# Three pads that move the operands of the MLP products in SBUF

## The chip, the cores and the metric

The kernel runs on one core of a Trainium2 chip. The metric is the device time of one execution in microseconds; three runs of the kernel before took 2766.51, 2768.69 and 2768.96 us, so the median is 2768.69 us. All times below come from these runs and from one profiled execution.

## The reference

Two transformer blocks follow each other on one sequence of 1024 tokens with 1024 channels, in float32. The first block adds to x the sum of three gated attention branches (sliding window, sparse with an exact top 256, and cross-attention to a memory of 256 tokens), then an MLP, and a norm. The second block is modulated by a conditioning vector; its mixer is a two-way mLSTM with four heads beside a multi-scale pooling, and it too ends in an MLP. The two MLPs are the part that the pads are named after:

```python
h = rmsnorm(x, g_mlp[l])
hid = jnp.square(jax.nn.relu(jnp.einsum("bsd,df->bsf", h, w_mlp_in[l])))
x = x + jnp.einsum("bsf,fd->bsd", hid, w_mlp_out[l])
...
h = _modulate(_rmsnorm(x, g_ffn[l]), sh2, sc2)
a = jnp.square(jax.nn.relu(jnp.einsum('bsd,df->bsf', h, w_ff1[l])))
x = x + gt2[:, None, :] * jnp.einsum('bsf,fd->bsd', a, w_ff2[l])
```

d is 1024 and f is 4096.

## The kernel before

Every large product is done in three: an operand is split into a high part (float32r) and the rest, and the kernel adds hi x hi, hi x lo and lo x hi in one PSUM bank. In `gemm_T` these are the lines L418, L419 and L420. A weight unit (128 contraction rows, 128 output channels, tiles wh and wl) is the stationary operand; the activations, transposed so that tokens lie along the free dimension, are the moving one, 512 tokens at a time. A moving operand is thus 128 partitions by 512 values of 4 bytes, 2048 bytes of each partition. The second mixer issues the same three products at L1301 to L1303 (`gemm2`), and the gates that are computed in advance, between the attention's steps, at L268 to L270.

The activations stand in these tiles: h_hi and h_lo, the normed input of a block or of an MLP, 8 channel blocks of 512 tokens, one pair for each half of the tokens (the first half in pool hA, the second in hB, or in hBp while hB holds the residual); hid_hi and hid_lo, the hidden layer of an MLP, rings of four tiles each in pool hidp; and for smaller products o_s, om and od (the outputs of the three attention branches), m (the merged branches) and y (the second mixer's output).

An MLP (`mlp`) goes in eight chunks of 512 hidden channels. In a chunk, four weight units give four hid tiles of both halves (8 channel blocks x 2 halves x 3 products each), and eight output blocks then take 4 x 2 x 3 products each from them. ScalarE takes the relu out of PSUM, VectorE squares it, and both split it; VectorE adds each output block into the residual stream x. Weights arrive by SP's DMA queue in tile wr and are split by ScalarE (L131) and VectorE or GpSimd (L132) into rings of three wh and wl tiles.

Pools are stacks: pools on the left side of SBUF grow upward from the constants (cst), hA and hB directly above; pools on the right (the weights' wp above all) grow downward. A pool that is opened takes the next free address, so whatever lies below a tile sets its address. Instructions are written out in a fixed order, and the tile framework puts the waits in by the tiles' addresses.

Of the kernel before, what the change touches and what calls it, by code (L numbers as in the profile page):

```python
# [19 lines left out]
P = 128  # L20
# [40 lines left out]
def block_kernel(ctx, tc, x, mem, positions, g_mix, w_in, b_gate, sinks, g_mem, w_mem_kv, w_proj_swa, w_proj_dsa,  # L61
# [65 lines left out]
    # ------------------------------------------------------------------ weights  # L127
# [12 lines left out]
    # ------------------------------------------------------------------ inputs needed first  # L140
# [6 lines left out]
    # ------------------------------------------------------------------ natural rmsnorm + transposes  # L147
# [32 lines left out]
    # ------------------------------------------------------------------ rope tables  # L180
# [52 lines left out]
    # ------------------------------------------------------------------ gates in advance, between the attention's steps  # L233
# [10 lines left out]
    def gates_ahead(todo):  # L244
        """tanh of half the gates' logits, into DRAM; a piece of three products at a time"""
# [55 lines left out]
    # ------------------------------------------------------------------ natural GEMM pieces  # L301
# [17 lines left out]
    def rope_nat(pool, acc, t, nh, dst=None):  # L319
        """acc: PSUM [P, nh*64] -> rotated [P, nh, 64] in SBUF"""  # L320
        av = acc.rearrange("p (h two j) -> p h two j", h=nh, two=2)
        a = pool([P, nh, 2, 32], tag="rp_a", bufs=2)
        V.tensor_tensor(a, av, cosT[:, t, :].unsqueeze(1).unsqueeze(1).to_broadcast([P, nh, 2, 32]), op=OP.mult)
        b = pool([P, nh, 2, 32], tag="rp_b", bufs=1)
        V.tensor_tensor(b[:, :, 0, :], av[:, :, 1, :], nsinT[:, t, :].unsqueeze(1).to_broadcast([P, nh, 32]),
                        op=OP.mult)
        V.tensor_tensor(b[:, :, 1, :], av[:, :, 0, :], sinT[:, t, :].unsqueeze(1).to_broadcast([P, nh, 32]),
                        op=OP.mult)
        if dst is None:
            G.tensor_tensor(a, a, b, op=OP.add)  # L330
            return a.rearrange("p h two j -> p h (two j)")
        G.tensor_tensor(dst.rearrange("p h (two j) -> p h two j", two=2), a, b, op=OP.add)

    def split_stack(st, src):
        """st [P, n, 2, 64]: the two parts of src [P, n, 64]"""
        A.copy(st[:, :, 0, :], src)
        V.tensor_tensor(st[:, :, 1, :], src, raw(st[:, :, 0, :]), op=OP.subtract)

    def stack_q(pool, q, nh):
        """[P, nh, 64] -> stacks [hi;lo] per head, still natural"""  # L340
        st = pool([P, nh, 2, 64], F32R, tag=f"stq{nh}", bufs=2)
        split_stack(st, q)
        return st

    def turn_q(pool, st, nh):
        """stacks of stack_q -> transposed: [128, nh, 128]"""
# [8 lines left out]
    def stack_k(pool, k, nh):  # L355
        """[P, nh, 64] -> per head [hi;hi;lo;lo], still natural"""
# [9 lines left out]
    def turn_k(sts, dst):  # L366
        """stacks of stack_k -> dst(h) = (hi, lo) each [128, 128], both duplicated over the two halves"""
# [9 lines left out]
    def pipeline(n, *stages):  # L377
        """stage s of item i is traced s rounds behind stage 0 of that item; (rounds, stage) for one of other length"""
        stages = [z if isinstance(z, tuple) else (n, z) for z in stages]
        for r in range(n + len(stages) - 1):  # L380
            for z in reversed(range(len(stages))):
                if 0 <= r - z < stages[z][0]:
                    stages[z][1] and stages[z][1](r - z)
# [5 lines left out]
    def attn_scale(pool, pv, rec):  # L389
        """pv PSUM [P, 4, 64] * rec [P, 4], natural"""  # L390
# [4 lines left out]
    def attn_turn(o, t, dst, dst_lo=None):  # L395
        """o of attn_scale -> transposed into dst [P, 2, S], tile t (in two parts with dst_lo)"""
# [12 lines left out]
    def gemm_T(accs, units, rhs, order=None, mid=None):  # L409
        """accs: PSUM banks, one per 512-token half; rhs(k, half) -> (hi, lo); order of the contraction; mid() is traced  # L410
        behind MID of its steps"""
# [18 lines left out]
    def gate_tanh(br, e, put, eng=None):  # L430
        """put(half): tanh of half the gate's logit; sigmoid(z) = (1 + tanh(z/2)) / 2"""
# [6 lines left out]
    # ------------------------------------------------------------------ DSA: index scores  # L438
# [14 lines left out]
    def mask(t, s0, n):  # L453
        """additive selection mask of query tile t; from tile 2 on it replaces the index scores"""
# [11 lines left out]
    def load_cols(r0, r1, eng, vecs):  # L466
        """rows r0..r1 of the vectors as columns"""
# [67 lines left out]
    def idx_x(t):  # L535
        """second half of the input, then the memory, behind the first products"""
# [18 lines left out]
    def mem_kv(r):  # L555
        """keys and values of the memory, in four steps"""
# [26 lines left out]
    # ------------------------------------------------------------------ DSA: exact top-k threshold, in the background  # L583
# [43 lines left out]
    # ------------------------------------------------------------------ memory attention  # L627
# [7 lines left out]
    def bg(n, after):  # L635
        """n steps of the selection, queued behind an instruction"""
# [63 lines left out]
    # ------------------------------------------------------------------ sliding-window attention  # L700
# [106 lines left out]
    # ------------------------------------------------------------------ gated projections of two branches  # L807
# [42 lines left out]
    # ------------------------------------------------------------------ DSA attention  # L850
# [68 lines left out]
    def dsa_drain(unit=None):  # L919
        """one step of the units behind: scores -> transposed -> products -> output"""  # L920
# [33 lines left out]
    # ------------------------------------------------------------------ gated projection of the third branch, merge  # L954
# [27 lines left out]
    # ------------------------------------------------------------------ transposed residual stream, its statistics  # L982
# [3 lines left out]
    class Stat:  # L986
        """sums of squares over the model dimension of w tokens, as columns [P, w / P] per gain"""
# [23 lines left out]
        def cols(self, short=False):  # L1011
            """rsqrt of the mean of the first sum as columns; short: the fewest steps one behind the other"""
# [17 lines left out]
    def spread(r):  # L1030
        """PSUM bank [P, 512]: column values [P, 4] of each token on every partition"""
# [5 lines left out]
    def out_proj(pool, w, rhs, upd, post, pre=lambda hf, e: None, order=range(DC), eng=lambda hf, e: None):  # L1037
        """traces post of the first half between products of the second; returns the two steps of the second's"""
# [30 lines left out]
    def make_h(pool, dst, src, rs, gain, shift=None):  # L1069
        """dst = src * gain * rs (+ shift), split; src(c), gain(c): APs"""  # L1070
# [17 lines left out]
    def x_cols(hf, e):  # L1088
        """columns e of the input, transposed into the residual stream"""
# [17 lines left out]
    hBp = Pool("hBp")  # L1107
    HT[1] = h_tiles(hBp)

    # ------------------------------------------------------------------ modulation vectors, in the background  # L1110
# [32 lines left out]
    def mlp(pool, w1, w2, upd, post, begin, tick=lambda: None, gains=None, each=lambda i, e: None,  # L1143
            parts=((0, 0, 512), (1, 0, 512))):
        """begin: two steps traced among the first products, which need the first half only; the last sums are taken
        over parts of the tokens, (half, first, number); post(part, statistics): a generator of two steps; each(part,
        e) is traced a product behind the last sum of block e"""
# [89 lines left out]
    def h2_half(hf, st):  # L1237
        """both norms between the blocks and the modulation: x * gsc2 * r1 * r2 + shift"""
# [37 lines left out]
    def big(pool, tag, bufs, shape=(P, S)):  # L1276
        """a tile of S values a partition, or a little more"""
# [9 lines left out]
    def unit2(m):  # L1287
        """weights of unit m; the ring holds three, each loaded when the last use of the third before it is traced"""
# [4 lines left out]
    def gemm2(ms, put):  # L1293
        """products of units ms, in pieces; put(i, half, bank) takes them"""
# [61 lines left out]
    # ------------------------------------------------------------------ mLSTM gates  # L1356
# [52 lines left out]
    # rows (direction, head, chunk) x position in the chunk  # L1409
# [72 lines left out]
    # ------------------------------------------------------------------ residual between the blocks, kept in DRAM  # L1482
# [7 lines left out]
    # ------------------------------------------------------------------ mLSTM heads  # L1490
# [9 lines left out]
    def rows_of(t_, d_, r0):  # L1500
        """rows r0..r0+7 on every partition: [P, 8, 128]"""
# [5 lines left out]
    def weights_of(hd, d_):  # L1507
        """exp of the log weights between the positions of a chunk, transposed"""
# [7 lines left out]
    def prepare(hd, d_):  # L1516
        """weighted scores, queries with their decay, weighted keys of a direction; the scores take the keys' place"""
# [18 lines left out]
    def mlstm(hd, hm, steps):  # L1536
        """both directions; steps(direction, i) traces other work behind each chunk"""
# [46 lines left out]
    # ------------------------------------------------------------------ centred multi-scale pooling  # L1584
# [47 lines left out]
    def hm_of(hd):  # L1632
        """the head's output: in the place of a pooled channel that is written later"""
# [42 lines left out]
    # ------------------------------------------------------------------ output projection of the second mixer  # L1676
# [13 lines left out]
    def pre_out2(hf, e):  # L1690
        """the residual and the second half's operand, a block at a time"""
# [16 lines left out]
    # ------------------------------------------------------------------ second MLP, last norm, output  # L1708
    hidp = Pool("hidp")
    ots = {}  # L1710
# [5 lines left out]
    def turn_out(i, e):  # L1716
        """block e of the output, scaled by its gain, with tokens on the partitions"""
# [63 lines left out]
```

## Time and profile before

| What | us |
|---|---|
| median of three runs | 2768.69 |
| span of the profiled execution | 2765.6 |
| TensorE matmuls busy in it | 2702.0 |
| VectorE busy | 1441.8 |
| ScalarE busy | 918.9 |
| GpSimd busy | 341.0 |

The span goes from the first to the last instruction of the program; the 3.1 us between it and the median of the runs lie around it. Busy time of an engine that others wait for counts, of others not. Matmuls overlap in the records: the duration of one (some 395 ns for 512 columns) is longer than the step from its start to the next one's, so steps are read from start times or from counts in a window.

### The profile page before, as it was taken

Reading aid. Unit: us, or ns where it says so; the run is one execution under the profiler, and the core shown is the slowest. Engines: PE = TensorE matmul, PEld = TensorE weight load, DVE = VectorE, ACT = ScalarE, POOL = GpSimd, SP = SyncE. Lnnn points to the kernel's source line nnn. Section 1 sums busy time; section 2 is a strip of 40 time slices with the busy share of each in tenths; the row PEclk is TensorE's granted clock in tenths of the full one; section 3 lists DMA queues with packets and bytes.
Section 4 is the critical chain, followed back from the end, with each engine's and each line's share of the span. In section 5 each row is a group of like instructions: output and inputs, shape, how many; then the busy total and the mean of one; then the engine's idle time right before and its main releaser. Section 6 shows DMA issues by size and latency. Waiting matters only on the chain.

```text
span 2765.6 us, 34329 instructions
## 1 busy us (share of the span) xinstructions
PE 2702.0 (98%) x13328; PEld 2228.3 (81%) x13328; DVE 1441.8 (52%) x2836; ACT 918.9 (33%) x1826; POOL 341.0 (12%) x337
## 2 busy tenths in 40 slices
PE   7999999999999999999999999999999999999997
PEld 6899987788878788888888777887888888888886
DVE  7686768824445534554453577556553333333335
ACT  6676754235334221112211332333431122111223
POOL 3011113320011000000000321111400000000006
PEclk9999999999999999999999999999999999999999
DMA  3121122311243313331231124221421111111123
GB/s 112 52 64 39 31 77 87 99 45 41 86 152 108 119 49 97 114 114 55 84 102 57 54 54 142 77 69 44 132 65 54 54 42 38 54 54 46 39 61 122
DMA packets 263735, 206.41 MB, mean 75 GB/s; under 512 B 9468, under 2 KB 239636, under 8 KB 263572
## 3 DMA queue, kind: packets, MB, share of 16 engines
q1 hardware_dynamic: 255108, 180.25, 21.6%
q10 hardware_dynamic: 8464, 23.96, 2.5%
q8 instruction: 105, 1.72, 0.3%
q14 instruction: 58, 0.48, 0.1%
HBM read 185.24 MB, written 18.94 MB: 74 GB/s over the span
## 4 chain that ended last, share of the span: by engine, by line
PE 71%; DVE 3%; DMA 2%; ACT 1%; issue 1%; POOL 1%; POOLq 0%; SPq 0%; ACTq 0%; DVEq 0%
PE mm L419 19%; PE mm L420 19%; PE mm L418 19%; PE mm L1301 2%; PE mm L1303 2%; PE mm L1302 2%; PE tp L911 1%; DVE st_acc L1006 1%; PE mm L899 1%; DMA adaw<-in_w_ada_dram 1%; ACT wh L131 0%; PE fl L268 0%; PE fl L270 0%; PE fl L269 0%; DVE wl L132 0%
## 5 line engine op out<-in xcount | busy, mean ns | idle before, releaser
L420 PE MATMUL mm<-h_hi,wl 128*128 128x512 f32 x1248 | 493.9, 396 | 1.1 <-POOL wl L132 1.1
L418 PE MATMUL mm<-h_hi,wh 128*128 128x512 f32 x1248 | 494.1, 396 | 0.6 <-ACT ft L277 0.6
L419 PE MATMUL mm<-h_lo,wh 128*128 128x512 f32 x1248 | 493.6, 395 | 0.0
L131 ACT CAST wh<-wr 128x1024 fp32r<-128x1024 f32 (+3 forms) x303 | 254.4, 840 | 711.6 <-PE mm L419 612.7
L419 PE MATMUL mm<-hid_lo,wh 128*128 128x512 f32 (+1 forms) x1056 | 411.6, 390 | 3.4 <-DVE hid_lo L1160 3.3
L418 PE MATMUL mm<-hid_hi,wh 128*128 128x512 f32 (+1 forms) x1056 | 413.5, 392 | 0.0
L420 PE MATMUL mm<-hid_hi,wl 128*128 128x512 f32 (+1 forms) x1056 | 411.1, 389 | 0.0
L1158 DVE TENSOR_TENSOR ml_q<-ml_r 128x512 f32<-128x512 f32 x128 | 88.0, 688 | 437.8 <-ACT ml_r L1156 437.8
L132 POOL TENSOR_TENSOR wl<-wr,wh 128x1024 fp32r<-128x1024 f32 (+5 forms) x60 | 124.5, 2078 | 1506.2 <-ACT wh L131 1492.5
L420 PEld LDWEIGHTS mm<-h_hi,wl 128*128 128x128 f32 x1248 | 234.4, 188 | 59.1 <-POOL wl L132 2.0
L418 PEld LDWEIGHTS mm<-h_hi,wh 128*128 128x128 f32 x1248 | 234.5, 188 | 57.4 <-ACT ft L277 0.8
L419 PEld LDWEIGHTS mm<-h_lo,wh 128*128 128x128 f32 x1248 | 234.5, 188 | 56.3
L132 DVE TENSOR_TENSOR wl<-wr,wh 128x1024 fp32r<-128x1024 f32 (+2 forms) x243 | 235.2, 968 | 50.7 <-ACT wh L131 46.8
L419 PEld LDWEIGHTS mm<-hid_lo,wh 128*128 128x128 f32 x1056 | 199.1, 189 | 49.4 <-DVE hid_lo L1160 4.9
L420 PEld LDWEIGHTS mm<-hid_hi,wl 128*128 128x128 f32 x1056 | 199.0, 188 | 44.9
L418 PEld LDWEIGHTS mm<-hid_hi,wh 128*128 128x128 f32 x1056 | 198.9, 188 | 44.6
L1156 ACT ACTIVATE ml_r<-mm 128x512 f32<-128x512 f32 x128 | 76.6, 598 | 468.8 <-PE mm L420 468.8
L1065 DVE SCALAR_TENSOR_TENSOR x<-mm,mod,x 128x512 f32<-128x512 f32 (+1 forms) x152 | 106.8, 722 | 233.6 <-PE mm L420 233.6
L1301 PE MATMUL mm<-h_hi,wh 128*128 128x512 f32 x320 | 133.0, 416 | 0.4 <-DVE kn L1334 0.4
L1303 PE MATMUL mm<-h_hi,wl 128*128 128x512 f32 x320 | 128.2, 400 | 2.9 <-DVE wl L132 2.9
L1302 PE MATMUL mm<-h_lo,wh 128*128 128x512 f32 x320 | 127.4, 398 | 0.0
L1063 DVE TENSOR_TENSOR h_hi<-mm,h_hi 128x512 f32<-128x512 f32 x72 | 49.6, 689 | 131.6 <-PE mm L420 131.6
(474 smaller groups left out, 4578.1 us busy)
## 6 DMA issues: line engine op xcount, KB each, us to landing
adaw<-in_w_ada_dram SPq DMA_DIRECT2D x48, 512.0 KB
wr<-in_w_ff_dram SPq DMA_DIRECT2D x44, 512.0 KB
wr<-in_w_in_dram SPq DMA_DIRECT2D x42, 512.0 KB
wr<-in_w_out_dram SPq DMA_DIRECT2D x32, 512.0 KB
wr<-in_w_mlp_in_dram SPq DMA_DIRECT2D x32, 512.0 KB
wr<-in_w_mlp_out_dram SPq DMA_DIRECT2D x56, 256.0 KB
wr<-in_w_ff_dram SPq DMA_DIRECT2D x56, 256.0 KB
wr<-in_w_in_dram SPq DMA_DIRECT2D x20, 256.0 KB
```

The source lines that it names most:

```text
L131: A.copy(hi, r)
L132: (eng or V).tensor_tensor(lo, r, raw(hi), op=OP.subtract)
L418: mm(a, hi, r_hi, start=(i == 0), stop=False)
L419: mm(a, hi, r_lo, start=False, stop=False)
L420: mm(a, lo, r_hi, start=False, stop=(i == n - 1))
L1063: V.tensor_tensor(d, a, d, op=OP.add)
L1065: V.scalar_tensor_tensor(d, a, scale[:, e:e + 1], d, op0=OP.mult, op1=OP.add)
L1156: A.activation(r, a, AF.Relu)
L1158: V.tensor_tensor(q, r, r, op=OP.mult)
L1301: mm(a, hi[:, k, :], r_hi, start=(k == 0), stop=False)
L1302: mm(a, hi[:, k, :], r_lo, start=False, stop=False)
L1303: mm(a, lo[:, k, :], r_hi, start=False, stop=(k == DC - 1))
```

## The change

Three tiles that nothing reads or writes are put into pools ahead of others: 8 values (32 bytes of a partition) at the end of cst, below hA; 192 values (768 bytes) in hBp, below the second half's h; and 64 values (256 bytes) in the second MLP's hidp, below gb and hid. Comments and docstrings are dropped in the same change, at equal line counts; the lines of the new kernel are one, two or three higher than those of before.

```diff
@@ inputs needed first
     def col(name, i):
         r0, _ = ROWS[name]
         return cols[:, r0 + i:r0 + i + 1]
 
+    cst([P, 8], tag="offA")
     hA = Pool("hA")
     hB = Pool("hB")
@@ after the first block's output projection
     drm.close()
     hBp = Pool("hBp")
+    hBp([P, 192], tag="offB")
     HT[1] = h_tiles(hBp)
@@ second MLP
     hidp = Pool("hidp")
+    hidp([P, 64], tag="offC")
     ots = {}
     gb_ = hidp([P, D], tag="gb")
```

The places of the moving operands of 512 columns, in bytes of a partition modulo 2048, as the two built programs lay them out, with the number of such products:

| moving operand | products | before | after |
|---|---|---|---|
| hid of the first MLP | 1536 | 1216 | 2016 |
| h, second half, in hBp (first MLP, second mixer) | 1272 | 1216 | 2016 |
| hid of the second MLP | 1440 | 1216 | 1504 |
| h in hA and hB, m, y, o_s, kd | 4968 | 1216 | 1248 |
| om | 96 | 1888 | 1888 |
| od | 96 | 2016 | 2016 |
| ki (index scores) | 48 | 1344 | 1376 |

The weights' rings stay where they were; their 512-byte rows start at 480, 992, 1504 and 2016. Each engine has the same instructions in the same order in both programs. One wait differs: the first kw of the second mixer (L1534, GpSimd) also waits for the transposes of st_acc (L1023), since its tile now overlaps that tile's place, and one DMA on SP's queue waits with one instruction where it had two.

## Rows read from the trace of the kernel before

**Rows 1.** The page: busy us, granted clock in 40 slices, chain of waits.
```profile
PE 2702.0 (98%) x13328; PEld 2228.3 (81%) x13328; DVE 1441.8 (52%) x2836; ACT 918.9 (33%) x1826; POOL 341.0 (12%) x337
...
PEclk9999999999999999999999999999999999999999
...
PE 71%; DVE 3%; DMA 2%; ACT 1%; issue 1%; POOL 1%; POOLq 0%; SPq 0%; ACTq 0%; DVEq 0%
PE mm L419 19%; PE mm L420 19%; PE mm L418 19%; PE mm L1301 2%; PE mm L1303 2%; PE mm L1302 2%; PE tp L911 1%; DVE st_acc L1006 1%; PE mm L899 1%; DMA adaw<-in_w_ada_dram 1%; ACT wh L131 0%; PE fl L268 0%; PE fl L270 0%; PE fl L269 0%; DVE wl L132 0%
```

**Rows 2.** Windows: us; PE, PEld, DVE, ACT, POOL busy; clock, DMA; last, PE alone.
```profile
200.00:376.00 176.00, 173.13 (x1278) 159.76 (x1277) 123.67 (x445) 118.05 (x330) 29.22 (x30) 1.00 0.16 47
...
890.00:1590.00 700.00, 696.53 (x3010) 560.30 (x3008) 323.54 (x430) 149.63 (x236) 27.49 (x14) 1.00 0.28 83
...
2110.00:2766.00 656.00, 640.74 (x2875) 520.24 (x2873) 244.98 (x345) 144.48 (x226) 48.27 (x33) 1.00 0.18 56
...
2200.00:2600.00 400.00, 400.00 (x1716) 1.00 0.16 47
```

**Rows 3.** Waits of TensorE, the longest: us in total, times, longest.
```profile
PE tp L1023 <- DVE st_acc L1008: 6.9, 3, 3.2
```

**Rows 4.** Groups by line and form: count, busy us, mean ns, idle before.
```profile
L418 PE MATMUL mm<-h_hi,wh 128*128 128x512 f32 x1248 | 494.1, 396 | 0.6 <-ACT ft L277 0.6
...
L418 PE MATMUL mm<-hid_hi,wh 128*128 128x512 f32 x992 | 394.2, 397 | 0.0
...
L1301 PE MATMUL mm<-h_hi,wh 128*128 128x512 f32 x320 | 133.0, 416 | 0.4 <-DVE kn L1334 0.4
...
L268 PE MATMUL fl<-h_hi,fh 128*128 128x512 f32 x160 | 68.6, 429 | 1.5 <-ACT fh L131 1.0 <-ACT ft L277 0.6
...
L419 PE MATMUL mm<-m_lo,wh 128*128 128x512 f32 x128 | 50.9, 398 | 0.0
...
L419 PE MATMUL mm<-y_lo,wh 128*128 128x512 f32 x128 | 50.7, 396 | 0.1
...
L419 PE MATMUL mm<-o_s,wh 128*128 128x512 f32 x64 | 25.3, 395 | 0.0
...
L419 PE MATMUL mm<-hid_lo,wh 128*128 128x256 f32 x64 | 18.0, 281 | 0.0
...
L419 PE MATMUL mm<-om,wh 128*128 128x512 f32 x32 | 13.1, 410 | 0.0
...
L419 PE MATMUL mm<-od,wh 128*128 128x512 f32 x32 | 12.5, 390 | 0.0
```

**Rows 5.** Tile od: duration ns min/median/max, first and last start us.
```profile
L418 PEld LDWEIGHTS mm<-od,wh x32: 187/188/189, 726.0 to 780.8; 128*128 128x128 f32 x32
L418 PE MATMUL mm<-od,wh x32: 389/389/395, 726.2 to 781.1; 128*128 128x512 f32 x32
```

**Rows 6.** Timeline of TensorE around od: start us, us, line.
```profile
725.99 0.40 PE L420 MATMUL mm<-h_hi,wl 128*128 128x512 f32 x1
...
726.45 0.39 PE L419 MATMUL mm<-od,wh 128*128 128x512 f32 x1
...
731.67 0.40 PE L418 MATMUL mm<-h_hi,wh 128*128 128x512 f32 x1
```

**Rows 7.** Timeline of TensorE around om.
```profile
398.16 0.39 PE L419 MATMUL mm<-om,wh 128*128 128x512 f32 x1
...
398.62 0.40 PE L418 MATMUL mm<-om,wh 128*128 128x512 f32 x1
398.86 0.40 PE L419 MATMUL mm<-om,wh 128*128 128x512 f32 x1
...
400.72 0.39 PE L418 MATMUL mm<-h_hi,wh 128*128 128x512 f32 x1
```

**Rows 8.** Timeline of POOL at kw, and of TensorE at the st_acc transposes.
```profile
1695.93 1.90 POOL L1534 TENSOR_TENSOR kw<-kn,wkn 128x1024 f32<-128x1024 f32 x1 [60.66 <-DMA row<-MR]
...
1630.18 1.29 PE L1023 MATMUL tp<-ident,st_acc 128*128 128x128 f32 x8
```

## The prediction

> **What bounds the kernel now.** I read the page from the top: the busy shares, the granted clock by slices, and the chain of waits [rows 1]. TensorE is busy 2702.0 of 2765.6 us, and 71% of the chain that ended last is TensorE's, 57 points of it in the three product lines L418, L419 and L420. So the time is close to the number of matmuls times the step from one matmul's start to the next. The windows by stage say where this is strictly so [rows 2]: in the first MLP (890 to 1590 us) TensorE is idle for 3.5 of 700 us, in the window of the output projection and second MLP (2110 to 2766 us) for 15, nearly all at its end, and even in the attention window (200 to 376 us) for only 2.9 of 176. VectorE has 323.5 of the first MLP's 700 us, ScalarE 149.6. [...] TensorE waits little for others: its longest wait in total is 6.9 us [rows 3].
>
> The step itself comes from counting. 400 us in the middle of the second MLP hold 1716 matmul records, two of them cut by the edges: 400 / 1715 = 233.2 ns [rows 2]. [...]
>
> **Does an address matter here?** The change adds no work, so everything hangs on this, and the trace has a comparison. Nearly all 512-column products read their moving operand at 1216 modulo 2048; two small ones don't: od, the third branch's projection (2016), and om, the memory branch's (1888). The groups by line and form show mean durations of 395 to 397 ns for h, hid and o_s, and 390 for od [rows 4]; od's minimum and median are both 389 [rows 5]. The page's note says that the ends are modelled, so I take the step as well: from 726.45 to 731.67 us are 23 steps, 5.22 / 23 = 227.0 ns [rows 6]. The stage does not explain it, since the h products on both sides of od's run take the usual 0.40 us [rows 6]. Nor does the shape: o_s has the same form, loop and weight units, and it has 395 to 397. The weight load is 188 ns for all of them and starts with the matmul before it (726.0 us in od's first, 725.99 the matmul before), so it is hidden in either step [rows 5, 6]. The one difference I can name is the place of the operand. Its price is 233.2 - 227.0 = 6.2 ns by steps and 396 - 389 = 7 ns by durations. I use 6.5.
>
> om at 1888 tells that not every other place is as good: from 398.16 to 400.72 us are 11 steps, 232.7 ns on average, and they are uneven, 398.62 to 398.86 being 240 ns [rows 7].
>
> **The change, part by part.** It issues no instruction: all five engines have the same instructions in the same order before and after. One wait moves. kw (L1534, POOL) now also waits for TensorE's transposes of st_acc; those run at 1630.18 us, and kw at 1695.93, held by a DMA until then [rows 8]. That wait is long over: 0. What is queued behind kw on POOL therefore is not delayed.
>
> The rest is places. Counting the 512-column products whose operand moves: 9216 ([rows 4] shows one of three lines each: 3 x (1248 + 992 + 320 + 160 + 128 + 128 + 64) = 9120, and 96 small ones of kd and of the 16-column gates).
> - To 2016: hid of the first MLP, 8 chunks x 8 blocks x 4 x 2 halves x 3 = 1536, and the second half of h in hBp, 1272 in the first MLP and the second mixer: 2808. This is od's own place: 2808 x 6.5 ns = 18.3 us.
> - To 1504: hid of the second MLP, 7 x 8 x 4 x 2 x 3 + 96 = 1440. No row has 512 columns at 1504. Bounds: od's step (9.4 us less) and h's step (0); beyond nothing, om's worst step of 240 ns (9.8 us more).
> - To 1248, by the first pad, which lifts all of the left side by 32 bytes: the other 4968 (h in hA and hB, m, y, o_s, kd). No row has 1248 either. Bounds: od's step (32.3 us less), h's (0), om's worst step on every one (4968 x 6.8 ns = 33.8 us more).
>
> For the last two I take od's step. What 2016, 1504 and 1248 share, and 1216 and 1888 do not, is that they lie 32 bytes below a multiple of 256. The weights lie there as well (480, 992, 1504 and 2016 modulo 2048 in the ring). So if what counts is the place modulo 256, or the place relative to the weights' modulo 256, all three are od's case. If it is modulo 512, only 2016 and 1504 are; modulo 2048, only 2016. The trace of before cannot separate these. The 192 products of 256 columns at the end (281 ns each, [rows 4]) I leave as they are, with nothing counted.
>
> Off the sum I take 3 us: 480 of the 4968 are pieces of gates slipped in between the attention's steps (L268 to L270, 3 x 160), where VectorE and ScalarE have 124 and 118 of 176 us [rows 2] and part of a shorter step can turn into a wait: I halve them, 1.5 us. The other 1.5 us is for products that follow a wait and don't step at full pace; this is a guess. Together 18.3 + 9.4 + 32.3 - 3 = 57 us. What would be late next is VectorE; with 323.5 us in a stage that shrinks from 700 to about 680 (3120 products x 6.5 ns = 20), it is not. The weights' DMAs have a share of 0.28 there and need no more than today plus 3%.
>
> Against the profiled span that is 2765.6 - 57 = 2708.6 us. The median of the runs, 2768.69, lies 3.1 us over the span, so the forecast is 2712 us.
>
> [...] od and o_s differ by 6 ns at addresses that are both multiples of 16 [rows 4]. [...] The weight load lies beside the matmul in both [rows 5]. [...]
>
> **The rivals.**
> - B, the period is longer than 256 bytes, and 1248 gains nothing or a part. For it: 1216 and 1248 are only 32 bytes apart, and od is a single place. Against it: nothing in the trace. Time: 18.3 + 9.4 = 27.7 less, 2741; with a third of the first pad's 32 us, 2730.
> - C, 2016 alone is good. A matmul of 512 columns reads 2048 bytes, so consecutive operands meet at one place modulo 2048, and a period of 2048 would be natural. Time: 2768.7 - 18.3 = 2750.
> - D, the change doesn't do what it says: od is faster for something else that I don't see. Against it: o_s, and the h products on both sides. Time: 2768.7.
> - E, slower: 1248 steps as om does at its worst. 1248 and 1888 both stand at an odd multiple of 32, where 1216 stands at a multiple of 64, and om's steps are uneven. Price 33.8 us against 27.7 us of gain at the two other places: 2768.7 + 6 = 2775. It decides from a step of 233.2 + 27700 / 4968 = 238.8 ns. Against it: om's average is 232.7, and od is itself at an odd multiple of 32.
>
> **How the numbers follow.** A (all three places as od's) 0.48, B 0.22, C 0.10, D 0.11, E 0.09. The forecast is A's 2712 us; A's own range, with 6.2 to 7 ns and 0 to 5 us lost, is 2704 to 2718. A, B and C together hold 0.80 and reach to C's 2750, with a few us for the spread of runs: 2703 to 2755. About 0.2% (5.5 us) is what a measurement of this kernel can tell from none: A, B and C are faster by more (0.80), D is within (0.11), E is slower (0.09).
>
> **What would show it.** If A holds, the mean of L418 on hid and on h falls from 396 to about 390, 400 us of the second MLP hold about 1760 matmuls, not 1716, and the first MLP takes about 680 us. In B, hid shows 390 and h in hA and hB 396, so the first MLP gains 15 us and the second only 9. In C, hid of the second MLP stays at 396. In D all stay. In E the durations of h spread out above 396, as om's do, and L418 on h has a mean over 400. The forecast is wrong as a whole if hid of the first MLP, at od's own place, keeps its 396.

## The result and the profile after

The kernel with the three pads takes 2722.04 us (median of four runs, 2720.92 to 2724.2) against 2768.82 us for the kernel before in the runs beside it: a ratio of 0.9835, 95% interval 0.9821 to 0.9849. That is 46.8 us less. The forecast was 57 us less; the time lies within the range, and case A of the prediction (all three places as good as od's) is the one that happened, at 82% of its size. A's own range, 2704 to 2718 us, was missed by 4 us; that it is A and not a part of B is told by the durations and steps below, not by the time.

The page of the profile after, its busy times, granted clock and chain, as in [rows 1]:

```profile
span 2720.9 us, 34328 instructions
...
PE 2654.3 (98%) x13328; PEld 2229.8 (82%) x13328; DVE 1440.9 (53%) x2836; ACT 919.8 (34%) x1826; POOL 342.1 (13%) x337
...
PEclk9999999999999999999999999999999999999999
...
PE 70%; DVE 4%; DMA 2%; ACT 1%; issue 1%; POOL 1%; POOLq 0%; SPq 0%; ACTq 0%; DVEq 0%
```

The matmuls are the same 13,328, and their busy time is 47.7 us shorter; no other engine's busy time moved by 2 us. The granted clock is 1.00 in the windows below, as in those of [rows 2], so the gain does not come from the clock; in one place, at the end of this section, the clock took about a microsecond back.

Windows of the profile after (us; then PE, PEld, DVE, ACT, POOL busy with instructions; clock, DMA share, GB/s): the attention, the first MLP, the stretch from the output projection to the end, and, with PE alone, 400 us of the second MLP. The second holds the same work as its window in [rows 2], shifted to where it now lies; the third holds 12 matmuls fewer than the one there:

```profile
200.00:376.00 176.00, 173.14 (x1274) 160.12 (x1273) 122.39 (x443) 117.07 (x328) 29.29 (x30) 1.00 0.16 45
...
886.80:1568.60 681.80, 677.34 (x3010) 559.90 (x3008) 322.82 (x430) 149.88 (x236) 27.36 (x14) 1.00 0.29 86
2084.70:2720.90 636.20, 621.32 (x2863) 518.03 (x2861) 243.75 (x344) 144.70 (x226) 48.33 (x33) 1.00 0.19 57
```
```profile
2150.00:2550.00 400.00, 400.00 (x1766) 1.00 0.17 50
```

The same 3010 matmuls of the first MLP take 681.8 us instead of 700. In 400 us of the second MLP there are 1766 matmuls instead of 1716, a step of 400 / 1765 = 226.6 ns. In the attention, 176 us hold 1274 matmuls, 4 fewer than before: there the change gained nothing that shows.

Groups by line and form of the profile after (count, busy us, mean ns, idle before), beside [rows 4]:

```profile
L419 PE MATMUL mm<-h_hi,wh 128*128 128x512 f32 x1248 | 486.5, 390 | 0.6 <-ACT ft L278 0.6
...
L419 PE MATMUL mm<-hid_hi,wh 128*128 128x512 f32 x992 | 388.0, 391 | 0.0
...
L1303 PE MATMUL mm<-h_hi,wh 128*128 128x512 f32 x320 | 131.8, 412 | 0.5 <-DVE kn L1336 0.5
...
L312 PE MATMUL mm<-wh,h_lo 128*128 128x256 f32 x256 | 72.5, 283 | 0.0
...
L269 PE MATMUL fl<-h_hi,fh 128*128 128x512 f32 x160 | 68.4, 427 | 1.4 <-ACT fh L131 1.0 <-ACT ft L278 0.4
...
L420 PE MATMUL mm<-m_lo,wh 128*128 128x512 f32 x128 | 50.4, 394 | 0.0
...
L419 PE MATMUL mm<-o_s,wh 128*128 128x512 f32 x64 | 25.0, 390 | 1.4 <-DVE gt L842 1.4
...
L419 PE MATMUL mm<-od,wh 128*128 128x512 f32 x32 | 12.4, 389 | 0.0
```

h, hid and o_s now have 390 or 391, od 389 as before; the second mixer's products lost 4 ns of 416, the gates' 2 of 429. A timeline of TensorE in the second MLP shows that the steps are also even, 0.22 or 0.23 us one after the other (start us, duration us):

```profile
2199.62 0.39 PE L421 MATMUL mm<-h_hi,wl 128*128 128x512 f32 x1
2199.85 0.39 PE L419 MATMUL mm<-h_hi,wh 128*128 128x512 f32 x1
2200.07 0.39 PE L420 MATMUL mm<-h_lo,wh 128*128 128x512 f32 x1
2200.30 0.39 PE L421 MATMUL mm<-h_hi,wl 128*128 128x512 f32 x1
...
2205.97 0.39 PE L419 MATMUL mm<-h_hi,wh 128*128 128x512 f32 x1
```

From 2199.62 to 2205.97 are 28 steps, 226.8 ns each.

Where the time went: both programs issue the same matmuls in the same order, so the start of each can be set against the start of the same one before. A product's gain is how much shorter the time from its start to the next one's has become, a wait in between included. Added up over the 9216 products whose operand moved, by stage, with what 6.5 ns each would be:

| products | number | gained, us | at 6.5 ns, us |
|---|---|---|---|
| both MLPs, the second mixer's output projection | 6337 | 39.4 | 41.2 |
| second mixer | 1070 | 2.9 | 7.0 |
| first block's merge and output projection | 566 | 2.1 | 3.7 |
| projections of the branches | 573 | 2.5 | 3.7 |
| gates among the attention's steps, sparse attention | 670 | 0.7 | 4.4 |
| together | 9216 | 47.6 | 59.9 |

Against these 47.6 us stand 1.8 us that products of 256 columns lost (most of them the attention's, L310 to L312), and 1.1 us at om's. The spans differ by 44.7 us, the medians by 46.8; the 2 us between lie within the spread of the runs.

om's place did not change, and its microsecond is the clock's. Twelve of its products follow a wait for ScalarE's gt, 4.4 us where it was 4.0. The granted clock falls to 0.50 while TensorE waits (at 521.22 us, before the change at 522.21), and stays there for 6.8 us where it stayed for 3.4, so that 14 matmuls instead of 7 run in it, with 427 ns from one start to the next. The two stretches, after and before (us; PE busy with matmuls; clock, DMA share, GB/s):

```profile
521.22:528.05 6.83, 5.93 (x14) 0.50 0.07 22
```
```profile
522.21:525.62 3.41, 2.84 (x7) 0.50 0.00 0
```

The kernel with the weights moved (below) waits 4.3 us there and has the 3.4 us of before, so the longer stretch is not a fixed price of the change.

### The profile page after: what moved, and what is told of

Read it like the earlier page. It is cut to its first block, busy times and chain, and to the rows that moved or that the text cites. A ratio compares the mean times of both kernels' runs of the same rounds, so it can differ in the third digit from the quotient of the medians.

```text
span 2720.9 us, 34328 instructions
## 1 busy us (share of the span) xinstructions
PE 2654.3 (98%) x13328; PEld 2229.8 (82%) x13328; DVE 1440.9 (53%) x2836; ACT 919.8 (34%) x1826; POOL 342.1 (13%) x337
## 4 chain that ended last, share of the span: by engine, by line
PE 70%; DVE 4%; DMA 2%; ACT 1%; issue 1%; POOL 1%; POOLq 0%; SPq 0%; ACTq 0%; DVEq 0%
PE mm L420 19%; PE mm L421 19%; PE mm L419 19%; PE mm L1303 2%; PE mm L1305 2%; PE mm L1304 2%; PE tp L912 1%; DVE st_acc L1007 1%; PE mm L900 1%; DMA adaw<-in_w_ada_dram 1%; DVE h_lo L1081 0%; ACT wh L131 0%; DMA xt<-in_x_dram 0%; DVE t L1074 0%; PE fl L269 0%
## 5 line engine op out<-in xcount | busy, mean ns | idle before, releaser
L421 PE MATMUL mm<-h_hi,wl 128*128 128x512 f32 x1248 | 486.1, 389 | 1.1 <-POOL wl L132 1.1
L419 PE MATMUL mm<-h_hi,wh 128*128 128x512 f32 x1248 | 486.5, 390 | 0.6 <-ACT ft L278 0.6
L420 PE MATMUL mm<-h_lo,wh 128*128 128x512 f32 x1248 | 485.7, 389 | 0.0
L420 PE MATMUL mm<-hid_lo,wh 128*128 128x512 f32 (+1 forms) x1056 | 405.5, 384 | 4.0 <-DVE hid_lo L1162 4.0
L419 PE MATMUL mm<-hid_hi,wh 128*128 128x512 f32 (+1 forms) x1056 | 407.4, 386 | 0.0
L421 PE MATMUL mm<-hid_hi,wl 128*128 128x512 f32 (+1 forms) x1056 | 405.1, 384 | 0.0
L419 PEld LDWEIGHTS mm<-h_hi,wh 128*128 128x128 f32 x1248 | 234.4, 188 | 49.7 <-ACT ft L278 0.8
L419 PEld LDWEIGHTS mm<-hid_hi,wh 128*128 128x128 f32 x1056 | 198.9, 188 | 38.5
L1303 PE MATMUL mm<-h_hi,wh 128*128 128x512 f32 x320 | 131.8, 412 | 0.5 <-DVE kn L1336 0.5
L1305 PE MATMUL mm<-h_hi,wl 128*128 128x512 f32 x320 | 126.9, 396 | 3.3 <-DVE wl L132 3.3
L1304 PE MATMUL mm<-h_lo,wh 128*128 128x512 f32 x320 | 126.2, 394 | 0.0
```

The source lines that it names most:

```text
L419: mm(a, hi, r_hi, start=(i == 0), stop=False)
L420: mm(a, hi, r_lo, start=False, stop=False)
L421: mm(a, lo, r_hi, start=False, stop=(i == n - 1))
L1303: mm(a, hi[:, k, :], r_hi, start=(k == 0), stop=False)
L1304: mm(a, hi[:, k, :], r_lo, start=False, stop=False)
L1305: mm(a, lo[:, k, :], r_hi, start=False, stop=(k == DC - 1))
```

## The experiments

Two theories fit the result. Theory 1: the moving operand's own place modulo 256 sets the step, and 224 is a good one. Theory 2: its place relative to the stationary operand's modulo 256 does, and equal is good. The weights lie at 224 modulo 256, so the change fits both.

**The first pad alone.**

```diff
+    cst([P, 8], tag="offA")
     hA = Pool("hA")
     hB = Pool("hB")
```

> Only the first pad: h, hid, y, o_s all at 1248 modulo 2048 (224 modulo 256, as the weights), so the MLPs lose the places 2016 and 1504. Theory 1 (the place of the moving operand modulo 256 decides, 224 is a good one) and theory 2 (the moving operand's place against the weights' modulo 256 decides, equal is good) both say as with all three pads: 2722 us, within 4, and an h or hid product of 390 ns mean in either MLP. The rival, that the period is 2048 and 2016 the better place, says that the 2808 products of the first MLP's hid and second-half h fall behind by up to 6.5 ns: 2740 us.

Measured: 2723.41 us, ratio to before 0.9834 (0.982 to 0.9849). Groups of its trace:

```profile
L420 PE MATMUL mm<-h_lo,wh 128*128 128x512 f32 x1248 | 485.7, 389 | 0.0
L419 PE MATMUL mm<-hid_hi,wh 128*128 128x512 f32 x992 | 387.5, 391 | 0.0
```

The whole gain comes from 32 bytes. With all left operands at 1248 the products have the same 389 to 391 ns as at 2016 and 1504, so 2016 is not the better place that a period of 2048 would make it, and the second and third pad add nothing.

**The second and third pad alone.**

```diff
     hBp = Pool("hBp")
+    hBp([P, 192], tag="offB")
...
     hidp = Pool("hidp")
+    hidp([P, 64], tag="offC")
```

> The second and third pad without the first: h of the first MLP's second half and hid at 1984, hid of the second MLP at 1472, everything else at 1216: all 192 modulo 256, against weights at 224. Theories 1 and 2: no gain, 2769 us within 4, 396 ns a product. The rival with a period of 512 or 2048 says that 1984 or 1472 differ from 1216: up to 28 us of gain if both are good (2741 us), 9 to 18 if one is.

Measured: 2767.43 us, ratio 0.9996 (0.9987 to 1.0006). That is what both theories say: 768 and 256 bytes are whole multiples of 256 and do nothing. With the first pad alone it leaves no period of 512 or 2048: 1248, 1504 and 2016 are equally good, 1216, 1472 and 1984 equally poor. hid at 1984 and 1472 has the old duration:

```profile
L418 PE MATMUL mm<-hid_hi,wh 128*128 128x512 f32 x992 | 394.3, 397 | 0.0
```

**The weights moved instead.** The left operands stay at 1216; the weights go down by 32 bytes to meet them.

```diff
+    wq = Pool("wq", side="right")
+    wq([P, 8], tag="offW")
     wp = Pool("wp", side="right")
-    for p_ in (cst, wp):
+    for p_ in (cst, wq, wp):
```

> No pad below the left operands: h, hid, y, o_s stay at 1216 (192 modulo 256). Instead 32 bytes on the other side push the weights' rings, the fills' weights, od and om down by 32: weights and od from 224 to 192 modulo 256. Theory 2 (relative place): moving and stationary operands agree again, so the gain is the one of the three pads, 2722 us within 5, an h product of 390 ns mean. Theory 1 (absolute place, 224 good and 192 bad): nothing gained on the left, and od (240 products with 6.5 ns) worse: 2769 to 2771 us, an h product of 396 ns.

Measured: 2722.2 us, ratio 0.9828 (0.9811 to 0.9844), the time of the change itself. Groups of its trace:

```profile
L421 PE MATMUL mm<-h_lo,wh 128*128 128x512 f32 x1248 | 485.7, 389 | 0.0
L420 PE MATMUL mm<-hid_hi,wh 128*128 128x512 f32 x992 | 387.8, 391 | 0.0
...
L313 PE MATMUL mm<-wh,h_lo 128*128 128x256 f32 x256 | 72.5, 283 | 0.0
...
L420 PE MATMUL mm<-od,wh 128*128 128x512 f32 x32 | 12.5, 389 | 0.0
```

h and hid stand at 1216, where they had 396 and 397 ns [rows 4], and now have 389 and 391. od moved from 224 to 192 modulo 256 together with the weights and kept its 389. Theory 1 falls, theory 2 holds: what counts is how the two operands lie to each other.

**Products alone, a map of places.** 36 sets of 96 matmuls back to back, in one kernel that does nothing else, run once, as the two other kernels of products alone were. The mean granted clock over the span is 0.994 in it, 0.993 and 0.992 in the two others. mv and st are tiles that begin at 0 modulo 256; w(s, i) and m(q, i) are slices of them that begin s and q bytes in.

```python
for i in R: mm(bk[i // 8 % 4], w(224, i), m(192, i), **a(i))  # L71
for i in R: mm(bk[i // 8 % 4], w(224, i), m(224, i), **a(i))  # L73
for i in R: mm(bk[i // 8 % 4], w(192, i), m(192, i), **a(i))  # L78
for i in R: mm(bk[i // 8 % 4], w(192, i), m(224, i), **a(i))  # L80
for i in R: mm(bk[i // 8 % 4], w(96, i), m(96, i), **a(i))  # L83
```

> A kernel of products alone (the reference is not computed): 36 sets of 96 matmuls back to back, weights loaded for each, with moving and stationary operand at chosen places modulo 256. Theory 1: the step depends on the moving place alone: 226.7 ns at 224 and 233.3 at 192 whatever the stationary place; so with the stationary operand at 192, moving 192 is 233 and moving 224 is 227. Theory 2: it depends on the difference: 227 ns at a difference of 0 (224/224, 192/192, 96/96), 233 at 32 bytes to either side, and the set of stationary 192 repeats that of stationary 224 shifted by 32 bytes. Theory 2 for 256 columns: differing places give the shorter step (117 ns against 120). Neither says what the other differences give; a step below 226.7 ns would be a place better than the change's.

Measured, for these five lines and one of 256 columns (duration ns min/median/max, first and last start us):

```profile
L71 PE MATMUL bk<-mv,st x96: 395/396/397, 339.3 to 361.5; 128*128 128x512 f32 x96
...
L73 PE MATMUL bk<-mv,st x96: 388/389/398, 383.5 to 405.1; 128*128 128x512 f32 x96
...
L78 PE MATMUL bk<-mv,st x96: 387/389/397, 494.1 to 515.6; 128*128 128x512 f32 x96
...
L80 PE MATMUL bk<-mv,st x96: 393/396/399, 538.1 to 560.3; 128*128 128x512 f32 x96
...
L83 PE MATMUL bk<-mv,st x96: 389/389/395, 604.9 to 626.4; 128*128 128x512 f32 x96
...
L88 PE MATMUL bk<-mv,st x96: 282/283/284, 716.5 to 727.9; 128*128 128x256 f32 x96
```

Moving 224 has 389 ns with the weights at 224 and 396 with them at 192; moving 192 the other way round. From 383.5 to 405.1 us are 95 steps, from 538.1 to 560.3 also: 227.4 and 233.7 ns, by rounded starts. The mean step of each set, from the exact starts, by the moving operand's place less the stationary one's, modulo 256 (which steps at a set's ends are left out changes it by some 0.1 ns):

| difference, bytes | 0 | 16 | 32 | 48 | 64 | 80 | 96 | 112 | 128 | 144 | 160 | 176 | 192 | 208 | 224 | 240 |
|---|---|---|---|---|---|---|---|---|---|---|---|---|---|---|---|---|
| step, ns | 226.8 | 231.6 | 233.3 | 233.3 | 229.0 | 231.1 | 233.4 | 231.1 | 232.3 | 233.3 | 234.2 | 231.1 | 233.3 | 234.7 | 233.3 | 226.7 |

The eight sets with the weights at 192 and the three at 96 give the row's values at their differences again, within 0.2 ns. Differences of 0 and 240 are the best; 4 bytes, a difference that is no multiple of 16, is the worst, 236.7, and 8 bytes has 233.2. The kernel before had 224, one of the poor ones, and the change brought it to 0. For 256 columns it is another row: 120.0 at 0 and at 128, 116.7 at 32, so a difference of 0 is not good for every shape. 384 columns step by 173.5 ns at 0 and at 224 alike.

**A difference of 64 in the whole kernel.**

```diff
+    cst([P, 24], tag="offA")
     hA = Pool("hA")
     hB = Pool("hB")
```

> One pad of 96 bytes below the left operands: they lie at 1312 (32 modulo 256), 64 bytes above the weights modulo 256, a difference that no kernel here has had. The map of products alone has 229.0 ns a step there, against 233.3 at the 224 of before and 226.8 at 0. Theory 2 (the difference modulo 256 sets the step, in this kernel as in the map): (233.3 - 229.0) / (233.3 - 226.8) = 0.66 of the 46 us that a difference of 0 brought: 2738 us, within 4, and an h product about 392 ns. The rival, that only a difference of 0 is special in the whole kernel and every other is as before: 2768 us.

Measured: 2736.02 us, ratio 0.9881 (0.9865 to 0.9898). The map gave 2738 for it. 400 us of its second MLP (as above), and groups of its trace, a product of the MLPs and one of the attention's with 256 columns:

```profile
2160.00:2560.00 400.00, 400.00 (x1749) 1.00 0.17 50
```
```profile
L419 PE MATMUL mm<-hid_hi,wh 128*128 128x512 f32 x992 | 391.6, 395 | 0.0
...
L312 PE MATMUL mm<-wh,h_lo 128*128 128x256 f32 x256 | 71.3, 279 | 0.0
```

The last group in the kernel before:

```profile
L311 PE MATMUL mm<-wh,h_lo 128*128 128x256 f32 x256 | 71.7, 280 | 0.0
```

The window's step is 400 / 1748 = 228.8 ns, where the map has 229.0. A difference that neither kernel has gives the part of the gain that the products alone foretold; that is the strongest support for theory 2. And the attention's products of 256 columns, in which the weights move and h is stationary, have 279 ns here, 280 before, 283 in the kernel after and in the one with the weights moved. Their median step is 117 ns before, at a difference of 32, 120 after, at 0, and 114 here, at 192.

**Products alone, among others.** Alternating places, the same weights again, 256 columns, bf16, and short products between long ones.

```python
for i in R: mm(bk[i // 8 % 4], w((224, 192)[i // 2 % 2], i), m(224, i), **a(i))  # L70
for i in R: mm(bk[i // 8 % 4], w(224, i // 4), m(224, i), **a(i))  # L73
for i in R: mm(bk[i // 8 % 4][:, :256], w(224, i), m(160, i, 256), **a(i))  # L83
for i in R: mm(bk[i // 8 % 4], u(0, i), v(32, i), **a(i))  # L88, bf16
# L95, L98: three of 512 columns, three of 128; q is 224 in L95, 0 in L98
for i in R: mm(bk[i // 8 % 4] if i % 6 < 3 else bk[i // 8 % 4][:, :128], w(224, i),
               m(q, i, 512 if i % 6 < 3 else 128), start=True, stop=True)
```

> Products alone again (the reference is not computed), 32 sets of 96. Which load contends: if the moving operand is slowed by the load of the next product's weights, then with the stationary place 224, 224, 192, 192 in turn and moving 224 the steps of 227 and 233 follow the next product's weights; if its own weights decide, they follow its own. In either case the mean is half way, 230 ns. The same stationary slice for four products: if its load is left out, no dependence on the place; if it is loaded again, 227 against 233 ns as before. 256 columns: 120 ns at differences of 0 and 128, 117 at 32 and 240 by the first map; open for the others, above all for 16, which decides whether moving the left operands by 16 bytes would be better than by 32. bf16: open; its moving rows are half as long, so if the bytes read count and not the columns, its places repeat otherwise. Groups of three products of 512 columns and three of 128: if gains add up, a group at moving 224 is 3 x 6.5 = 19.5 ns shorter than at moving 0; if products among short ones lose theirs, as the second mixer's and the gates' seem to, under 10.

Measured for four of the sets, bf16 at differences of 0 and 32, and the mixed groups at moving 224 and 0:

```profile
L86 PE MATMUL bk<-bm,bs x96: 379/379/389, 327.4 to 348.0; 128*128 128x512 bf16 x96
...
L88 PE MATMUL bk<-bm,bs x96: 379/379/379, 368.9 to 389.4; 128*128 128x512 bf16 x96
...
L95 PE MATMUL bk<-mv,st x96: 220/334/580, 513.8 to 530.2; 128*128 128x512 f32 x48, 128*128 128x128 f32 x48
...
L98 PE MATMUL bk<-mv,st x96: 221/334/452, 557.4 to 573.7; 128*128 128x512 f32 x48, 128*128 128x128 f32 x48
```

Four answers, and one question that stayed open:

- With short products between them, the long ones lose their gain: a group of three and three takes 1026 ns at moving 224 and 1030 at 0 by its steps, 4 ns instead of the 19.5 of full gains; one and one, 342.8 and 343.0. The steps from long to long in the threes are 231 to 233 ns even at a difference of 0. Products of 128 columns alone step by 111.6 or 111.7 ns at either place.
- bf16 does not see the place: 215.8 ns at each of nine moving places, with the weights at 0.
- 256 columns go down to 113.3 ns at a difference of 192 and 113.7 at 112; moving 240, a difference of 16, has 118.7.
- The same slice of weights for four products is loaded again each time (96 loads in the set), at 226.7 and 233.3 ns as before.
- What stayed open is which product's weights count: with weights at 224, 224, 192, 192 in turn and moving 224, the four kinds of product step by 229.8 to 231.3 ns, near the half way that was expected, but following neither their own weights nor the next product's. With the weights at 224 and 192 in turn the mean is 233.4, not half way; with the moving operand in turn and the weights at 224 the steps are 225 and 235, and the mean is 229.9. So a product's step depends on more than the difference of its own two places.

**Products alone, fewer columns of weights loaded.**

```python
for i in R: mm(bk[i // 8 % 4], w(224, i)[:, :128], m(224, i), **a(i))  # L69; L70 at moving 0
for i in R: mm(bk[i // 8 % 4][:16], w(224, i)[:, :16], m(224, i), **a(i))  # L81; L82 at moving 0
```

> Products alone (the reference is not computed), with 128, 64, 32 and 16 columns of stationary operand loaded for each, at differences of 0, 32, 128 and 224 bytes for 512 columns of moving operand and 0, 32, 112 and 192 for 256. [...] The rival, that the place of the operands costs by itself, whatever is loaded beside it: 226.8 and 233.3 ns stay at every width.

Measured, at 16 columns of weights:

```profile
L81 PE MATMUL bk<-mv,st x96: 387/389/397, 336.9 to 358.6; 128*16 128x512 f32 x96
...
L82 PE MATMUL bk<-mv,st x96: 389/389/398, 358.9 to 380.4; 128*16 128x512 f32 x96
```

The step does not stay at 226.8 and 233.3 ns at every width. With 128 columns loaded the steps are 226.7 and 233.3 ns at differences of 0 and 32; with 64 they are 229.9 and 230.9, with 32 231.7 and 233.1, and with 16 it is turned round, 228.9 and 226.7, though a load takes 94 ns there instead of 188. The gap between the two places is thus 6.6, 1.0, 1.4 and -2.2 ns: which difference is the good one depends on how many columns are loaded and, by the sets of 256 (120.0 ns at 0, 116.7 at 32), on how many are streamed. No set of 512 float32r columns had a mean step under 226.6 ns.

## Why the prediction was right, and where its size was off

- **The comparison of od with h and o_s was the right one, and its price too.** 6.5 ns were read from od; the MLPs' and the output projection's 6337 products gained 39.4 us, 6.2 ns each, and the map has 233.3 - 226.8 = 6.5. The signs that it named for A came true as well: 390 ns, 1766 matmuls for some 1760, 681.8 us for some 680.
- **All three places are od's case.** "Modulo 256" was argued from what 2016, 1504 and 1248 have in common; the first pad alone and the other two alone show it. Rivals B and C fall with them, D with the gain, E with 1248's even steps.
- **Own place or relative place was left open; it is the relative one.** The kernel with the weights moved has the whole 46 us (2722.2 us against 2768.08) without moving one left operand, and h and hid at 1216 have 389 and 391 ns in it. How the two operands meet, no run shows. Own place or relative, the sum was the same here by luck: the weights and od happened to share 224.
- **The step that failed is the sum's last: "Off the sum I take 3 us".** The gross sum of 60 us was measured as 47.6, so 12.3 should have come off, and 2.9 more for products that got slower. The prediction halved 480 gate pieces and guessed 1.5 us for the rest. In fact 2879 products outside the MLPs and the second output projection gained 2.8 ns each, 8.2 us instead of 18.7. The reason that it gave, that a shorter step turns into a wait, covers little of this: all of TensorE's idle time grew by 2.9 us, from 63.6 to 66.5. The products alone show another: there nothing waits for another engine, and the long ones lose most of their gain between short ones all the same. The traces of the two kernels agree. Counted by how many products of 512 columns follow each other with no other product between, from the exact starts, the 7494 in rows of more than 24 gained 6.0 ns each; the 1722 in rows of at most 24 gained 1.7 ns each, 2.9 us instead of the 11.2 of full gains (2.4 us with the first pad alone, 3.0 with the weights moved). That makes short neighbours the likely cause of some 8 of the 12.3 us. It is not isolated: the short rows also lie in the stages with the most waits, and no experiment took the short products out of the second mixer.
- **"With nothing counted" failed for 256 columns.** The prediction set only the last 192 at nothing and did not list the attention's 768 at all, whose moving operand (the weights) stayed put. But their stationary operand is h, which moved, and their difference went from 32 to 0: 117 to 120 ns, with 280 others of 256 columns in that stage 1.7 us lost. The kernel with the weights moved has the same 120, the one at a difference of 64 has 114.
- **The wait of kw cost nothing and VectorE did not become the bound**, as said: kw is still held by its DMA, with POOL idle for 60.3 us before it where it was 60.7. In one place a shorter step did turn into a wait: the first block's projections (L419) wait 6.7 us for ScalarE's gt where they waited 5.0 (L418). The other three kernels that got faster have 6.1 to 7.5 there, the one with the second and third pad alone has 4.6. The stretch at half the clock behind it was in no term of the prediction's sum.

Two things follow. One pad of 32 bytes does what the three do (2723.41 and 2722.04 us, within the spread of the runs). And the attention's 256-column products would step by 113 ns at a difference of 192, by the products alone 768 x 6.7 = 5.1 us less than after. The kernel at a difference of 64 has them at 192, and by the exact starts they take 3.5 us less there than in the kernel after; but h is also the moving operand of the gates and projections, which want 0. No kernel here has both.

## What to carry to other kernels

In a kernel bound by float32r matmuls, look at the place of the moving operand against the stationary one, modulo 256: for products of 512 columns with 128 x 128 weights, equal places step by 227 ns where 32 bytes of difference step by 233. Find it by a group whose operand lies elsewhere, as od did, and then move one side by a pad of a few values; price only the runs of long products (6.0 ns each here), not those with short ones between them (1.7 ns). Other shapes have other good differences, and bf16 at 512 columns showed none, so measure the shape at hand.

## What was not expected of the hardware

- The mean steps of 226.7 and 233.3 ns differ by 6.6 ns, those of 113.3 and 120.0 by 6.7, and all four are near whole multiples of 6.67 ns: 34, 35, 17 and 18 times. Sets between them have uneven steps, such as 230, 238, 224, 232 at a difference of 112. Where this grain comes from is not known.
- For the same 512 columns bf16 takes 215.8 ns at every place tried, 11 ns less than the best of float32r.
- With 16 columns of weights loaded, a difference of 32 is good (226.7 ns) and 0 is not (228.9). Why the good difference moves with the size of the load stayed open.
